# A hybrid decoder step: operands of the chunked recurrence built for four chunks at a time, with wider scans and a decode step by columns

## The chip, the cores and the metric

The kernel runs on one core of a Trainium2 chip. The metric is the device time of one execution in microseconds (us); the kernel before takes 1289.98 us, the median of three runs.

The engines of the core are named as the profile does: PE is TensorE (matmul) and PEld its weight loads, DVE is VectorE, ACT is ScalarE, POOL is GpSimd, SP is SyncE, which here issues most transfers. Each works its own queue in order; semaphores hold an instruction until what it needs is done.

## The reference

One step of a layer with 1024 prompt tokens and 8 decode tokens, model width 1024, 2048 mixed channels. Everything goes through one input projection; three branches read it, and one output projection closes it:

- A: dilated attention, 12 heads of 64, with the three patterns (128,1), (512,4), (2048,16) combined by their softmax denominators; for the decode tokens against a cache of 2048 rows.
- B: a spatial gating unit with chunks of 128 tokens and 8 groups.
- C: a gated linear recurrence of 6 heads with a state of 128 x 128. This is the branch that the change touches:

```python
def body(S, xs):
    qc, kc, vc, gc = xs
    G = jnp.cumsum(gc, axis=1)
    o_inter = jnp.einsum('bchk,bhkv->bchv', qc * jnp.exp(G), S)
    diff = G[:, :, None] - G[:, None, :]
    D = jnp.exp(jnp.where(tri, diff, -jnp.inf))
    A = jnp.einsum('bthk,btshk,bshk->bths', qc, D, kc)
    o = o_inter + jnp.einsum('bths,bshv->bthv', A, vc)
    G_last = G[:, -1]
    S_new = jnp.exp(G_last)[..., None] * S + jnp.einsum(
        'bshk,bshv->bhkv', kc * jnp.exp(G_last[:, None] - G), vc)
    return S_new, o
```

G is the running sum of the logarithms of the forget gate f, k is one minus f. For a decode token the same is one update per head, `S_new = f * S + k v`, and `o = q S_new`.

## The kernel before

The stages run in the order attention, recurrence (`hgrn`), gating unit (`sgu`), output projection. A scheduler that works with estimated times orders the instructions of each engine, so projections of a later head stand among the recurrence of an earlier one. A matmul of the projections is done as three products of rounded parts (high, low); every matmul has the line of the helper `mm` (L100).

`hgrn` goes through three pairs of heads. `c_proj_i` (PSUM tiles `pi`, drained by ACT into V), `c_proj_qf` (tiles `pc`: the part for f drained by ACT at L572, that for q by DVE in `gate`, L152) and `c_proj_z` (tiles `pcz`, drained at L152) are projections. They share two PSUM buffers, so the third product group waits for the drain of the first. `c_head` then works on one head with 1024 tokens in eight chunks of 128:

- It forms G by a running sum for each chunk (L651, eight scans against a tile of ones, which start anew in each chunk), H = G - ln k, eG = exp(G) q (L659).
- For each half of four chunks it transposes k exp(G_last - G) (L667, tile kT), and for each pair of chunks it calls `levels`: for the block widths 32, 8 and 2 a tile T of the `s2` pool with 640 columns, 256 of key operands K (L628) and 384 of query operands Q (L630 differences, L631 exponential on ACT, L633 copy of decays dec on ACT, L634 to L636 products on DVE). The function also makes `last` (L639, L640).
- PE multiplies K and Q of the levels into small blocks of a PSUM tile (`lv`), DVE puts them together in `cmat` (L703 to L710), and PE multiplies this and the state into the output `po`; DVE updates the state S (L721).

`s2` has six tiles. Two calls of `levels` (a half) fill them, and attention uses them for the rounded parts plo and phi of its probabilities (L473, L487). `c_step` is the decode step of a head: for four decode tokens at a time it loads v to all partitions (vb) and the state (ss), and DVE does three multiplications or additions over 512 columns (L752 to L754). `decode` is the attention over the cache for a pair of heads and has its own DVE work on tiles dk, dsc and dmb. GpSimd forms the low parts of the weights (L193).

`sgu` uses one `s2` tile for a bias (bT), and the output projection loads eight tiles of mixed channels y at its start, six of them into `s2`.

## Time and profile before

| what | us |
|---|---|
| median of three runs (1288.97 to 1293.23) | 1289.98 |
| the profiled execution | 1287.74 |
| its span, first to last instruction | 1286.0 |
| TensorE busy (94%) | 1215.2 |
| VectorE busy (71%) | 916.5 |
| ScalarE busy (50%) | 644.2 |
| GpSimd busy (22%) | 285.5 |

The profile is of one execution. A share of busy time is an average over four stages; matmuls are pipelined, so busy time is not peak rate. "Idle before" names the time that an engine stood still ahead of an instruction and what released it. [...]

### The profile page before, as it was taken

How to read it: one execution, taken by the hardware profiler on the slowest of the kernel's cores; microseconds unless marked ns; L12 is line 12 of the kernel's file. 1: busy time of each engine (PE TensorE's matmuls, PEld its weight loads, DVE VectorE, ACT ScalarE, POOL GpSimd, SP SyncE). 2: the span in 40 equal slices, each digit the busy share in tenths (PEclk: the TensorE clock that was granted, in tenths of full speed). 3: DMA queues.
4: the chain of work that ended last, by engine and by line, in shares of the span. 5: the costliest groups of instructions: out<-in, count | busy, mean ns of one | idle time of the engine just before them, and what ended most of it. 6: DMA issues, size and time to landing. Idle time of an engine off the chain costs nothing.

```text
span 1286.0 us, 27698 instructions
## 1 busy us (share of the span) xinstructions
PE 1215.2 (94%) x10610; PEld 1129.3 (88%) x10610; DVE 916.5 (71%) x2427; ACT 644.2 (50%) x1486; POOL 285.5 (22%) x272
## 2 busy tenths in 40 slices
PE   4899989999999999998999989997999999999998
PEld 3899979999899988997888878887889899899998
DVE  5844778668776685879888897889796534664643
ACT  4444444745347554565445554565443242454543
POOL 3532112312123121121011111111011254122221
PEclk9999989999899999999999989999899999999999
DMA  6151032312223123124343424424353224621110
GB/s 234 24 148 54 14 105 62 111 51 59 57 78 107 38 84 89 29 64 107 91 134 96 117 61 134 132 66 106 95 153 95 86 68 134 203 79 46 62 47 29
DMA packets 165045, 114.17 MB, mean 89 GB/s; under 512 B 13945, under 2 KB 158993, under 8 KB 164913
## 3 DMA queue, kind: packets, MB, share of 16 engines
q1 hardware_dynamic: 157520, 110.28, 29.4%
q10 hardware_dynamic: 6816, 1.54, 0.6%
q8 instruction: 83, 1.36, 0.5%
q0 software_dynamic: 576, 0.58, 0.3%
q14 instruction: 50, 0.40, 0.1%
HBM read 84.47 MB, written 22.09 MB: 83 GB/s over the span
## 4 chain that ended last, share of the span: by engine, by line
PE 75%; DVE 15%; DMA 4%; issue 3%; ACT 2%; SPq 0%; POOL 0%; ACTq 0%; DVEq 0%; POOLq 0%
PE po L100 15%; PE pqk L100 10%; PE pv L100 9%; PE paz L100 5%; PE pi L100 5%; PE st L100 4%; PE pbu L100 4%; PE pc L100 4%; PE pbz L100 4%; PE pbv L100 3%; PE pcz L100 2%; PE s L100 2%; DMA dk<-in_cache_k_dram 2%; DVE T L628 2%; DVE T L630 1%
## 5 line engine op out<-in xcount | busy, mean ns | idle before, releaser
L100 PE MATMUL pqk<-wh_qk,h 128*128 128x256 f32 x768 | 157.4, 294 | 5.8 <-ACT h L233 3.0
L100 PE MATMUL pc<-h,wh_cqf 128*128 128x344 f32 x576 | 141.6, 326 | 11.3 <-DVE cz L152 8.0
L100 PE MATMUL po<-woh,yh 128*128 128x256 f32 x512 | 144.1, 282 | 0.5 <-ACT yh L1027 0.5
L100 PE MATMUL po<-woh,yl 128*128 128x256 f32 x512 | 144.2, 282 | 0.0
L100 PE MATMUL po<-wol,yh 128*128 128x256 f32 x512 | 143.4, 280 | 0.0
L100 PEld LDWEIGHTS pqk<-wh_qk,h 128*128 128x128 f32 x768 | 127.8, 197 | 12.3 <-ACT h L233 4.3
L100 PE MATMUL pqk<-wl_qk,h 128*128 128x256 f32 x384 | 113.0, 294 | 0.0
L100 PEld LDWEIGHTS pc<-h,wh_cqf 128*128 128x128 f32 x576 | 100.4, 190 | 14.0 <-DVE cz L152 8.8
L100 PEld LDWEIGHTS po<-woh,yl 128*128 128x128 f32 x512 | 96.2, 188 | 3.0 <-issue 1.7
L100 PEld LDWEIGHTS po<-woh,yh 128*128 128x128 f32 x512 | 96.3, 188 | 2.3 <-ACT yh L1027 2.3
L100 PEld LDWEIGHTS po<-wol,yh 128*128 128x128 f32 x512 | 96.5, 188 | 0.0
L437 DVE CUSTOM_DVE_ANT_0 s<-s,masks 128x512 f32<-128x512 f32 (+2 forms) x144 | 77.6, 578 | 22.7 <-PE s L100 21.7
L100 PE MATMUL pc<-h,wl_cqf 128*128 128x344 f32 x288 | 93.7, 327 | 0.0
L100 PE MATMUL pi<-wh_ci,h 128*128 128x256 f32 x384 | 77.5, 295 | 0.8 <-DVE T L635 0.8
L100 PEld LDWEIGHTS pqk<-wl_qk,h 128*128 128x128 f32 x384 | 75.9, 198 | 1.8 <-issue 0.7
L100 PE MATMUL pv<-wh_v,h 128*128 128x256 f32 x384 | 75.3, 287 | 0.3 <-DVE ss L164 0.3
L100 PE MATMUL pcz<-h,wh_cz 128*128 128x344 f32 x288 | 72.2, 330 | 2.3 <-DVE q L152 2.3
L100 PE MATMUL paz<-h,wh_az 128*128 128x344 f32 x288 | 69.0, 323 | 0.0
L1028 DVE TENSOR_TENSOR yl<-yb,yh 128x512 fp32r<-128x512 f32 x44 | 30.3, 691 | 53.3 <-ACT yh L1027 53.3
L100 PEld LDWEIGHTS pi<-wh_ci,h 128*128 128x128 f32 x384 | 63.5, 198 | 2.7 <-issue 2.4
L100 PEld LDWEIGHTS pv<-wh_v,h 128*128 128x128 f32 x384 | 61.8, 193 | 1.9 <-issue 1.2
L1027 ACT CAST yh<-yb 128x512 fp32r<-128x512 f32 x64 | 39.6, 620 | 43.4 <-PE po L100 43.4
(379 smaller groups left out, 3581.6 us busy)
## 6 DMA issues: line engine op xcount, KB each, us to landing
wro<-in_w_out_dram SPq DMA_DIRECT2D x32, 256.0 KB
wr_qk<-in_w_in_dram SPq DMA_DIRECT2D x48, 128.0 KB
wr_cqf<-in_w_in_dram SPq DMA_DIRECT2D x48, 128.0 KB
dk<-in_cache_k_dram SPq DMA_DIRECT2D x24, 192.0 KB
dv<-in_cache_v_dram SPq DMA_DIRECT2D x24, 192.0 KB
xt<-in_x_prompt_dram SPq DMA_DIRECT2D x8, 512.0 KB
xr<-in_x_prompt_dram SPq DMA_DIRECT2D x32, 128.0 KB
out_o_yp_dram<-xr SPq DMA_DIRECT2D x32, 128.0 KB
```

The source lines that it names most:

```text
L100: nc.tensor.matmul(out, lhsT=lhsT, rhs=rhs, start=start, stop=stop)
L437: nc.vector.tensor_tensor_reduce(out=ps[:, :w], in0=ps[:, :w], in1=nmask[:, S - n + c:S - n + c + w], op0=ALU.add, op1=ALU.max, scale=1.0, ...
L628: nc.vector.tensor_tensor(K.rearrange("p (n w) -> p n w", w=w), g3[:, :, w - 1:w].to_broadcast([P, 4 * n, w]), h3, ALU.subtract)
L630: nc.vector.tensor_tensor(Q[:, 0:3], g4[:, 1:4], g4[:, 0:3, :, w - 1:w].to_broadcast([P, 3, n, w]), ALU.subtract)
L1027: nc.scalar.copy(yh[:, sl, :], y)
L1028: (nc.gpsimd if piece == 0 else nc.vector).tensor_tensor(yl[:, sl, :], y, yh[:, sl, :].bitcast(F32), ALU.subtract)
```

## The change

`levels` takes a half (four chunks) in one call: its tiles have 1280 columns, twice as wide, and each of its instructions works on twice the columns. `lasts` keeps the part that still goes by pairs. The pool `s2` has three tiles of double width in place of six, so attention takes one tile for its two parts, and bT moves to the pool of large tiles (16 buffers). The running sum goes over two chunks with a mask that is 0 at the first column of each chunk in place of the tile of ones. In `c_step`, ACT multiplies vb by a scalar per partition, one decode token at a time, and DVE does the rest as one instruction for each token. The loads of y are five, three of them for two tiles.

```diff
-N_BIG, N_S2, N_S2B, N_PQ, N_W, N_WL, N_GT, N_RAW, N_E = 16, 6, 2, 5, 4, 4, 2, 6, 3
+N_BIG, N_S2, N_S2B, N_PQ, N_W, N_WL, N_GT, N_RAW, N_E = 16, 3, 2, 5, 4, 4, 2, 6, 3
...
-                    plo = s2(f"pl{nm}", F32R)
+                    pl2 = s2(f"pl{nm}", F32R, (P, 2, 512))
+                    plo, phi = pl2[:, 0], pl2[:, 1]
...
-                    phi = s2(f"ph{nm}", F32R)
...
-        def levels(nm, b, q, f, G, H):
+        def levels(nm, b, q, G, H):
...
-                n = 64 // w
-                t = s2(f"T{nm}_{li}", shape=(P, 640))
-                K = t[:, 0:256]
-                Q = t[:, 256:640].rearrange("p (b n w) -> p b n w", b=6, w=w)
+                n = P // w
+                t = s2(f"T{nm}_{li}", shape=(P, 1280))
+                K = t[:, 0:512]
+                Q = t[:, 512:1280].rearrange("p (b n w) -> p b n w", b=6, w=w)
...
-                nc.scalar.activation(t[:, 0:448], t[:, 0:448], AF.Exp)
-                dec = small(f"dec{nm}_{li}", 2 * n, tag="dec").rearrange("p (j n) -> p j n", j=2)
+                nc.scalar.activation(t[:, 0:896], t[:, 0:896], AF.Exp)
+                dec = small(f"dec{nm}_{li}", 2 * n, tag="dec", bufs=1).rearrange("p (j n) -> p j n", j=2)
...
-            for c in range(NT):
-                cs = slice(c * P, (c + 1) * P)
-                nc.vector.tensor_tensor_scan(G[:, cs], ones, G[:, cs], 0.0, ALU.mult, ALU.add)
-                if c % 4 == 3:
-                    cs = slice((c - 3) * P, (c + 1) * P)
+            for c in range(0, NT, 2):
+                cs = slice(c * P, (c + 2) * P)
+                nc.vector.tensor_tensor_scan(G[:, cs], rmask, G[:, cs], 0.0, ALU.mult, ALU.add)
+                if c % 4 == 2:
+                    cs = slice((c - 2) * P, (c + 2) * P)
...
+                T = levels(f"{h}_{half}", b, q, G, H)
                 for c0 in (0, 2):
                     g0 = half * 4 + c0
-                    T, last = levels(f"{h}_{g0}", slice(g0 * P, (g0 + 2) * P), q, f, G, H)
+                    last = lasts(f"{h}_{g0}", slice(g0 * P, (g0 + 2) * P), q, f)
...
-                nc.vector.tensor_tensor(vb, vb, qs[:, 2, bs, None].to_broadcast([P, 4, P]), ALU.mult)
-                nc.vector.tensor_tensor(ss, ss, qs[:, 1, bs, None].to_broadcast([P, 4, P]), ALU.mult)
-                nc.vector.tensor_tensor(ss, ss, vb, ALU.add)
+                for b_ in range(4):
+                    b = 4 * b4 + b_
+                    nc.scalar.activation(vb[:, b_], vb[:, b_], AF.Copy, scale=qs[:, 2, b:b + 1])
+                    nc.vector.scalar_tensor_tensor(ss[:, b_], ss[:, b_], qs[:, 1, b:b + 1], vb[:, b_], ALU.mult, ALU.add)
...
-            bT = s2("bT", shape=(P, 4, P))
+            bT = wk("bT", (P, 4, P))
...
+            for i, n in ((0, 2), (2, 1), (3, 1), (4, 2), (6, 2)):
+                y = s2(f"y{i}", shape=(P, 2, 4, P)) if n == 2 else ee(f"y{i}", (P, 1, 4, P))
```

The order of the instructions moves with it. In the names below the digit behind the letters is the head; T2_4_0 is head 2, pair of chunks from chunk 4, first level, and after the change T2_1_0 is head 2, second half, first level.

VectorE, up to where it drains the second q projection of head 3 (pc3_0_1), which stands among the recurrence of head 2, before:

```order
L582 SCALAR_TENSOR_TENSOR f3_9467<-ft3_2_9557,f3_9467 128x344
L628 TENSOR_TENSOR T2_6_1_9225<-G2_8905,H2_8907 128x256
L630 TENSOR_TENSOR T2_6_1_9225<-G2_8905 128x192
L628 TENSOR_TENSOR T2_6_2_9234<-G2_8905,H2_8907 128x256
L630 TENSOR_TENSOR T2_6_2_9234<-G2_8905 128x192
L703 COPY_PREDICATED cmat_6252<-cmat_6252,lv2_2_9053 128x3x2x8
L640 TENSOR_TENSOR T2_6_q_9243<-f2_8498,q2_8499 128x8x16
L938 TENSOR_REDUCE dmb2_9380<-pmx2_9378 16x1
L156 TENSOR_TENSOR q3_9468<-q3_9468,qt3_0_9585 128x344
L703 COPY_PREDICATED cmat_6252<-cmat_6252,lv2_0_8968 128x2x8
L634 TENSOR_TENSOR T2_4_0_9130<-T2_4_0_9130,q2_8499 128x192
L152 TENSOR_SCALAR q3_9468<-pc3_0_1_9591 128x344
```

The same place after the change; the first row is the drain of the first q projection (pc3_0_0):

```order
L152 TENSOR_SCALAR q3_9242<-pc3_0_0_9334 128x344
L581 SCALAR_TENSOR_TENSOR ft3_0_9325<-k3_9243,f3_9241 128x344
L636 TENSOR_TENSOR T2_0_2_8774<-T2_0_2_8774,dec2_0_2_8778 128x256
L581 SCALAR_TENSOR_TENSOR ft3_1_9328<-k3_9243,f3_9241 128x344
L947 TENSOR_REDUCE dmb2_9154<-pmx2_9152 16x1
L582 SCALAR_TENSOR_TENSOR f3_9241<-ft3_0_9325,f3_9241 128x344
L582 SCALAR_TENSOR_TENSOR f3_9241<-ft3_1_9328,f3_9241 128x344
L948 COPY dmb2_9154<-dmb2_9154 16x128
L581 SCALAR_TENSOR_TENSOR ft3_2_9331<-k3_9243,f3_9241 128x344
L582 SCALAR_TENSOR_TENSOR f3_9241<-ft3_2_9331,f3_9241 128x344
L583 SCALAR_TENSOR_TENSOR k3_9243<-k3_9243,lb1_377,f3_9241 128x1032
L152 TENSOR_SCALAR q3_9242<-pc3_0_1_9365 128x344
```

Before, twenty-nine instructions lie between the two drains, among them twelve operands (L628, L630) of the second half of head 2; after the change ten, and none of these.

VectorE, up to the last drain of the gate projection (pcz1_1_2) at the start of head 2, before:

```order
L628 TENSOR_TENSOR T2_0_2_8956<-G2_8905,H2_8907 128x256
L630 TENSOR_TENSOR T2_0_2_8956<-G2_8905 128x192
L640 TENSOR_TENSOR T2_0_q_8965<-f2_8498,q2_8499 128x8x16
L628 TENSOR_TENSOR T2_2_0_9023<-G2_8905,H2_8907 128x256
L630 TENSOR_TENSOR T2_2_0_9023<-G2_8905 128x192
L628 TENSOR_TENSOR T2_2_1_9032<-G2_8905,H2_8907 128x256
L630 TENSOR_TENSOR T2_2_1_9032<-G2_8905 128x192
L628 TENSOR_TENSOR T2_2_2_9041<-G2_8905,H2_8907 128x256
L630 TENSOR_TENSOR T2_2_2_9041<-G2_8905 128x192
L640 TENSOR_TENSOR T2_2_q_9050<-f2_8498,q2_8499 128x8x16
L659 TENSOR_TENSOR eG2_8906<-eG2_8906,q2_8499 128x1024
L152 TENSOR_SCALAR cz1_1_8716<-pcz1_1_2_8872 128x344
```

And after the change; the first row is the drain in front of it:

```order
L152 TENSOR_SCALAR cz1_1_8538<-pcz1_1_1_8663 128x344
L725 SCALAR_TENSOR_TENSOR S1_6_7894<-S1_5_7839,eL1_7574,ls1_6_7845 128x128
L628 TENSOR_TENSOR T2_0_0_8756<-G2_8727,H2_8729 128x512
L628 TENSOR_TENSOR T2_0_1_8765<-G2_8727,H2_8729 128x512
L630 TENSOR_TENSOR T2_0_1_8765<-G2_8727 128x384
L628 TENSOR_TENSOR T2_0_2_8774<-G2_8727,H2_8729 128x512
L660 COPY eL2_8740<-eG2_8728 128x8
L630 TENSOR_TENSOR T2_0_2_8774<-G2_8727 128x384
L643 TENSOR_TENSOR T2_0_q_8783<-f2_8320,q2_8321 128x8x16
L643 TENSOR_TENSOR T2_2_q_8841<-f2_8320,q2_8321 128x8x16
L725 SCALAR_TENSOR_TENSOR S1_7_7898<-S1_6_7894,eL1_7574,ls1_6_7845 128x128
L152 TENSOR_SCALAR cz1_1_8538<-pcz1_1_2_8694 128x344
```

Eleven narrow operands, of which eight are shown, and the product eG2 stood between the two drains; now five wide ones do, with two updates of the state of head 1, and eG2 stands behind.

ScalarE, where head 2 ends and head 3 begins, before (pdt2s is the cache step, V2_0 and V2_1 drain `pi`):

```order
L602 COPY V2_1_10234<-pi2_0_10235 128x256
L602 COPY V2_0_10233<-pi2_1_10286 128x256
L602 COPY V2_1_10234<-pi2_1_10286 128x256
L724 ACTIVATE csq2_0_9109<-po2_0_8937 128x512
L737 COPY pdt2s_9431<-pda2_9392 128x256
L728 ACTIVATE csq2_0_9109<-pn2_0_9112,eps_69 128x512
L670 COPY kT2_1_9127<-pk2_1_9117 128x512
```

And after the change:

```order
L741 COPY pdt2s_9205<-pda2_9166 128x256
L758 ACTIVATE vb3_0_9784<-vb3_0_9784,qs3_9429 128x128 x4
L758 ACTIVATE vb3_1_9801<-vb3_1_9801,qs3_9429 128x128 x4
L642 COPY T3_0_q_9490<-q3_9242 128x8x32
L642 COPY T3_2_q_9548<-q3_9242 128x8x32
L602 COPY V2_0_9959<-pi2_1_10012 128x256
L602 COPY V2_1_9960<-pi2_1_10012 128x256
```

The eight multiplications of the decode step (two rows of four) now stand here, ahead of two drains of `pi`, which came ahead of the copy pdt2s before.

## Rows read from the trace of the kernel before

**Rows 1.** The page, busy us of each engine, share of the span, instructions.
```profile
PE 1215.2 (94%) x10610; PEld 1129.3 (88%) x10610; DVE 916.5 (71%) x2427; ACT 644.2 (50%) x1486; POOL 285.5 (22%) x272
```

**Rows 2.** Windows by stage: attention with its lead-in, recurrence, and the rest. Columns: stretch, its length, then busy us and (instructions) of PE, PEld, DVE, ACT, POOL; granted clock, DMA share, GB/s.
```profile
0.00:500.00 500.00, 464.38 (x3462) 431.75 (x3463) 350.32 (x895) 254.89 (x562) 123.78 (x139) 0.97 0.29 82
540.00:960.00 420.00, 388.82 (x4147) 354.54 (x4146) 363.50 (x1003) 227.67 (x540) 69.14 (x64) 0.96 0.38 105
960.00:1286.00 326.00, 321.96 (x2739) 304.69 (x2738) 174.32 (x458) 141.54 (x346) 86.29 (x64) 1.00 0.27 85
```

**Rows 3.** Timeline of PE from 540 to 960 us, the rows with over 1 us of idle time ahead. Columns: start, us, engine, line, operation, tiles, shapes, count, and in brackets the idle time ahead and what ended it.
```profile
582.21 0.73 PE L100 MATMUL pc<-h,wh_cqf 128*128 128x344 f32 x2 [2.66 <-DVE cz L152]
...
613.08 0.23 PE L941 MATMUL pmb<-ident,dmb 16*128 16x16 f32 x1 [3.43 <-DVE dmb L939]
...
652.00 0.58 PE L100 MATMUL pc<-h,wh_cqf 128*128 128x344 f32 x2 [2.19 <-ACT V L602]
...
684.29 0.59 PE L100 MATMUL pcz<-h,wh_cz 128*128 128x344 f32 x2 [1.84 <-DVE q L152]
...
727.39 0.58 PE L100 MATMUL pc<-h,wh_cqf 128*128 128x344 f32 x2 [3.02 <-DVE cz L152]
...
754.83 1.89 PE L100 MATMUL pss_ci<-wr_ci,hs 128*8 128x256 f32 x16 [3.68 <-DVE q L152]
...
830.77 0.71 PE L100 MATMUL po<-cmat,V 128*128 128x128 f32 x4 [1.23 <-DVE cmat L710]
...
870.30 0.58 PE L100 MATMUL pc<-h,wh_cqf 128*128 128x344 f32 x2 [2.29 <-DVE cz L152]
...
897.44 1.90 PE L100 MATMUL pss_bv<-wr_bv,hs 128*8 128x256 f32 x16 [3.66 <-DVE q L152]
...
942.27 0.49 PE L100 MATMUL po<-cmat,V 128*128 128x128 f32 x2 [2.08 <-DVE cmat L710]
```

**Rows 4.** Windows of 20 us, columns as in rows 2: the first and the last of the seven from 540 to 960 us whose granted clock is under 1.00.
```profile
580.00:600.00 20.00, 17.79 (x114) 16.77 (x114) 17.33 (x47) 9.53 (x27) 0.00 (x0) 0.91 0.59 148
...
900.00:920.00 20.00, 19.42 (x159) 18.06 (x160) 14.99 (x58) 8.46 (x19) 0.00 (x0) 0.83 0.29 88
```

**Rows 5.** Timeline of DVE at the start of head 0 and of head 2: the scans, and a run of operands up to a drain.
```profile
568.03 2.63 DVE L651 TENSOR_TENSOR_SCAN G<-ones,G 128x128 f32<-128x128 f32 x8 [1.12 <-ACT G L648]
...
723.67 0.42 DVE L628 TENSOR_TENSOR T<-G,H 128x256 f32<-128x256 f32 x1
724.01 0.35 DVE L630 TENSOR_TENSOR T<-G 128x192 f32<-128x192 f32 x1
724.28 0.42 DVE L628 TENSOR_TENSOR T<-G,H 128x256 f32<-128x256 f32 x1
...
725.69 1.22 DVE L659 TENSOR_TENSOR eG<-eG,q 128x1024 f32<-128x1024 f32 x1
726.82 0.51 DVE L152 TENSOR_SCALAR cz<-pcz 128x344 f32<-128x344 f32 x1
```

**Rows 6.** Timeline of DVE from the drain of one q projection of head 3 to the next.
```profile
742.66 0.51 DVE L152 TENSOR_SCALAR q<-pc 128x344 f32<-128x344 f32 x1
...
750.24 1.27 DVE L640 TENSOR_TENSOR T_q<-f,q 128x128 f32<-128x128 f32 x1
...
751.64 1.38 DVE L156 TENSOR_TENSOR q<-q,qt 128x344 f32<-128x344 f32 x1
...
753.02 1.33 DVE L634 TENSOR_TENSOR T<-T,q 128x192 f32<-128x192 f32 x1
754.27 0.50 DVE L152 TENSOR_SCALAR q<-pc 128x344 f32<-128x344 f32 x1
```

**Rows 7.** Timeline of POOL in the same stretch.
```profile
750.00 4.13 POOL L193 TENSOR_TENSOR wl_ci<-wr_ci,wh_ci 128x512 fp32r<-128x512 f32 x3 [26.67 <-ACT wh_ci L192]
```

**Rows 8.** The five lines of operands on DVE by line: count, duration in ns (min/median/max), first and last start, shape; under them the first of the five as a group (busy us, mean ns of one, idle time before).
```profile
L628 DVE TENSOR_TENSOR T<-G,H x72: 404/418/1520, 574.5 to 959.7; 128x256 f32<-128x256 f32 x72
L630 DVE TENSOR_TENSOR T<-G x72: 330/351/1444, 570.6 to 960.1; 128x192 f32<-128x192 f32 x72
L634 DVE TENSOR_TENSOR T<-T,q x72: 281/348/1406, 585.6 to 966.4; 128x192 f32<-128x192 f32 x72
L635 DVE TENSOR_TENSOR T<-T,dec x72: 202/212/1205, 587.3 to 967.1; 128x64 f32<-128x64 f32 x72
L636 DVE TENSOR_TENSOR T<-T,dec x72: 230/280/1378, 590.0 to 967.9; 128x128 f32<-128x128 f32 x72
...
L628 DVE TENSOR_TENSOR T<-G,H 128x256 f32<-128x256 f32 x72 | 34.1, 477 | 1.2 <-PE lv L100 1.2
```

**Rows 9.** By line, columns as in rows 8: a decode multiplication and the state update on DVE; on ACT an activation with 128 columns and an operand per partition, the exponentials of the levels and the copies of decays.
```profile
L754 DVE TENSOR_TENSOR ss<-ss,vb x12: 680/686/737, 544.5 to 933.1; 128x512 f32<-128x512 f32 x12
...
L721 DVE SCALAR_TENSOR_TENSOR S<-S,eL,ls x42: 326/346/350, 592.4 to 996.1; 128x128 f32<-128x128 f32 x42
...
L667 ACT ACTIVATE ki<-H,G x48: 386/393/412, 572.2 to 956.0; 128x128 f32<-128x128 f32 x48
...
L631 ACT ACTIVATE T<-T x72: 558/577/592, 575.4 to 960.5; 128x448 f32<-128x448 f32 x72
...
L633 ACT COPY dec<-T x72: 178/218/256, 582.1 to 965.5; 128x4 f32<-128x4 f32 x24, 128x16 f32<-128x16 f32 x24, 128x64 f32<-128x64 f32 x24
```

**Rows 10.** Waits of PE in the whole span: us in total, times, longest.
```profile
PE s L100 <- DMA QQ<-QQ: 6.9, 3, 2.4
```

More of the change, by code (lines that the diff above doesn't have):

```diff
@@ L636, in levels, with lasts @@
                 nc.vector.tensor_tensor(Q[:, 4:6], Q[:, 1:4:2], dec[:, 0:1, :, None].to_broadcast([P, 2, n, w]), ALU.mult)
-                T.append((K.rearrange("p (c s) -> p c s", c=2), t[:, 256:640].rearrange("p (b c s) -> p c b s", b=6, c=2)))
+                T.append((K.rearrange("p (c s) -> p c s", c=4), t[:, 512:1280].rearrange("p (b c s) -> p c b s", b=6, c=4)))
+            return T
+        def lasts(nm, b, q, f):
             last = ee(f"T{nm}_q", (P, 8, 48))
@@ L641, in levels, with c_head @@
                                                        for x in (f, q)), ALU.mult)
-            return T, last
-        def c_head(h, q, f, kk, qw, V, z, At, lmask, dmask):
+            return last
+        def c_head(h, q, f, kk, qw, V, z, At, lmask, dmask, rmask):
             G, eG, H = (wk(f"{n}{h}") for n in ("G", "eG", "H"))
@@ L766, in hgrn @@
             nc.gpsimd.memset(cm[:, 512:640], 0.0)
+            rmask = cm[:, 872:1000].bitcast(BF16)
+            nc.gpsimd.memset(rmask, 1.0)
+            nc.gpsimd.memset(rmask.rearrange("p (c s) -> p c s", c=2)[:, :, 0:1], 0.0)
             At = [(cm[:, 256 * j:256 * j + 256], cm[:, 512 + 64 * j:576 + 64 * j]) for j in range(2)]
@@ L987, in out_proj @@
             y_v = y_d.rearrange("(k p) s -> p k s", p=P)
-            YT = [s2(f"y{i}", shape=(P, 4, P)) if i < 6 else ee(f"y{i}", (P, 4, P)) for i in range(8)]
-            for i, y in enumerate(YT):
-                nc.sync.dma_start(y, y_v[:, 4 * (i % 3):4 * (i % 3) + 4, (i // 3) * P:(i // 3 + 1) * P])
+            YT = [None] * 8
+            for i, n in ((0, 2), (2, 1), (3, 1), (4, 2), (6, 2)):
+                y = s2(f"y{i}", shape=(P, 2, 4, P)) if n == 2 else ee(f"y{i}", (P, 1, 4, P))
+                nc.sync.dma_start(y.rearrange("p a k s -> p (a k) s"),
+                                  y_v[:, 4 * (i % 3):4 * (i % 3) + 4 * n, (i // 3) * P:(i // 3 + 1) * P])
+                YT[i:i + n] = [y[:, j] for j in range(n)]
             W0 = load_wo(0)
```

8 lines of the change are left out of this document (4 added, 4 removed).

## The prediction

> **What bounds the kernel now.** I read the totals first, then the same by stage, then what ends TensorE's idle time in the stage that the change rewrites. Over the whole span TensorE is busy for 1215.2 of 1286.0 us [rows 1], so only 71 us can be won without removing products, and no product is removed here. By stage [rows 2]: attention (up to 500 us) leaves 36 us idle, and the change leaves its work as it is; the recurrence (540 to 960 us) leaves 31 us, with VectorE busy for 363.5 of 420; what follows leaves 4 us, so an edit there is worth nothing as long as its transfers stay early. The gain has to come out of the recurrence.
>
> There TensorE's long gaps have a pattern [rows 3]. In each even head there are two: one where a projection product waits for VectorE to take the gate projection out of PSUM (2.66, 3.02, 2.29 us), and some 30 us later one where TensorE waits for VectorE around the q projections (3.43 us for dmb of the cache step in head 0; 3.68 and 3.66 us for a drain of q in heads 2 and 4). Odd heads have one each, and the transition to head 2 one that ScalarE ends: 2.19, 1.84, 1.23, 2.08 us. VectorE works its queue in order, and the drain of a projection stands behind operands of the recurrence. [...]
>
> **Operands of a level.** Five VectorE lines, each 72 times, become 36 times at double width: 180 instructions fewer, the same elements. What an instruction costs besides its elements: by durations, two of 256 columns against one of 512 are 2 x 0.418 - 0.686 = 0.15 us [rows 8, 9]; by the pitch of a run without waits, 0.34 and 0.27 us for 256 and 192 columns, hence 0.06 us [rows 5]. So the saving is 11 to 27 us; I take the middle, since operands that wait for ScalarE show their whole duration and the others only the pitch. [...]
>
> **Scans.** Eight of 128 columns run in 2.63 us [rows 5], 0.33 us each; four of 256 save four times the same 0.06 us in six heads, 1.5 us, and 3 us if the whole fixed part counts.
>
> **Decode step.** Three multiplications of 0.69 us [rows 9] twelve times, 25 us, become 48 instructions of 128 columns with a scalar per partition. The nearest row, the state update, takes 0.346 us [rows 9], and by pitch and columns it would be 0.20: 10 to 17 us. VectorE saves 8 to 15 us. ScalarE takes over 48 multiplications, by the nearest row 0.393 us each [rows 9], 19 us. It loses half of its 72 exponentials (0.577) and copies (0.218), whose fixed parts I leave uncounted; it is busy for 227.7 of 420 us [rows 2], so the time itself hides. The wait does not quite: the first of four now holds ScalarE until its load lands, and in head 3 the drains of pi stand right behind eight of them, as the order of ScalarE shows. TensorE then has one more projection of 48 products to do, 5.7 us at 0.12 us apiece by the last stage [rows 2], against 8 x 0.39 = 3.1 us. I price it at nothing, and at 3 us in each of six heads if the load is late.
>
> VectorE loses 21 to 45 us in all, of 363.5.
>
> **Where it falls.** The order of VectorE shows what TensorE feels. Between the drains of the first and second q projection before there are 742.66 to 754.27 = 11.6 us [rows 6], mostly operands of the *next* half written ahead into the second set of tiles. With one set these have to stand behind the drain. Twelve instructions of 0.34 or 0.27 us (3.7 us) and three that a GpSimd subtraction stretches to 1.3 us (4 us) leave this interval: more than the gap of 3.7 us that ends there. So **term a**: the three second gaps, 3.43 + 3.68 + 3.66 = 10.8 us. Ahead of the gate drain eleven narrow operands (6 x 0.34 + 5 x 0.27 = 3.4 us) and the product eG (1.13 us by pitch [rows 5]) become five wide ones (3 x 0.60 + 2 x 0.47 = 2.7 us, estimated from the pitch): 1.8 us less in each of three gaps. **Term b**: 5.4 us. **Term c**: the low clock follows the gaps that go; I take two thirds of 15.6 us, 10.4. **Term d**: the four other gaps, 7.3 us, of which a third, 2.4, because the queue in front of them is shorter by about that share. Together 29.0 us.
>
> **What it costs.** The second set of tiles is gone: the first operand of a half waits until TensorE has read the last product of the half before (levels now reuse all three tiles). From there to the first product that uses them lie 0.60 + 0.47 us, an exponential of under 2 x 0.577, then 0.47 + 0.20 + 0.33 us: about 3 us. TensorE has projections to do meanwhile: the order puts most of a projection group between the halves. I charge a quarter of twelve halves, 9 us, with 0 and 36 us as ends. The attention pairs of tiles, formerly six single ones, hold the same three groups; its order moves a little, and the three waits for copied queries (6.9 us [rows 10]) may grow or shrink by 3 us: nothing taken. bT takes one of sixteen large buffers: four vraw, four U, wn and bT leave six, before it was seven, and three of the four pairs of tiles for the first output weights fit either way. The loads of y become five instead of eight, off any wait that TensorE shows: nothing.
>
> **Sum.** 29.0 - 9 = 20 us off 1287.74 us, the profiled execution (its span and 1.74 us around it), gives 1267.7. That execution lies 2.24 us under the median of the three runs, so the forecast is 1267.7 + 2.2 = 1270 us.
>
> **Rivals.** *The port, not the count.* An instruction of 192 columns took 1.33 us and one of 128 took 1.27 us while GpSimd ran three subtractions in 4.13 us [rows 6, 7]; the longest subtraction of G and H took 1.52 us against a median of 0.418, and the mean is 0.477 [rows 8]. Taken alike for five lines, 360 x 0.06 = 21 us is spent so. It goes with GpSimd's instructions, which stay, so none of it is in my saving; and if the wide operands just meet them elsewhere, ahead of the drains, half of a and b and 3 us of c remain, against 5 of the 9 us charged: 5.4 + 2.7 + 3 - 5 = 6 us, 1284. [...]
>
> *One set of tiles decides.* If projections do not fill the pause between halves, the 3 us above are paid in all twelve, 36 us against 29: slower, 1297. It turns at 29 / 12 = 2.4 us a half. For it: TensorE already ran out of covered work in every head. Against it: it ran out because drains were late, not for want of projections, and these now come earlier.
>
> *The gaps only move.* VectorE was 87% busy in the stage; if TensorE waits for other drains instead, 1290. [...]
>
> **How the numbers follow.** Forecast (1262 to 1279) 0.48; port 0.18; gaps move 0.12; one set of tiles 0.13; everything 0.09. The first, second and last are faster by over 0.3% (3.9 us, about what a measurement of this kernel can tell from no change): 0.75. Same 0.12, slower 0.13. The range leaves out the slower rival and half of the last: 1250 to 1291.
>
> **What would show it.** Right: in the stage VectorE's busy time falls by 21 to 45 us, the waits for q and dmb behind even heads are gone, the granted clock is 1.00 in most windows, the recurrence ends some 20 us sooner. Wrong: new waits of TensorE for operands T or for cmat at the start of second halves; ScalarE idle for vb with drains behind it; the same shortfall of clock in other places; or a gain that appears outside the recurrence, which none of these terms explains.

## The result and the profile after

The changed kernel takes 1302.87 us, the median of nine runs (1294.2 to 1306.59), against 1288.97 for nine runs of the kernel before: a ratio of 1.0104, with a 95% interval of 1.0078 to 1.013. It is slower, outside the range of the forecast. The profiled execution took 1301.46 us, 13.7 more than the profiled one before. Executions of one program differ by nearly as much: of the nine after, the one with the highest granted clock over its span (0.983) took 1294.2 us, the eight others (0.972 to 0.975) 1299.2 to 1306.59 us. What a profile shows of idle time and clock is therefore one sample of its kernel. The granted clock is the share of its full clock that the profile shows TensorE to have had; in both profiles it was 1.00 or 0.50 at a time: before, it was 0.50 from 897 to 906 us and 1.00 from 908 to 912.

The first part of the page, which answers to [rows 1]:

```profile
PE 1227.6 (94%) x10610; PEld 1135.6 (87%) x10610; DVE 887.2 (68%) x2235; ACT 652.8 (50%) x1462; POOL 289.5 (22%) x274
```

VectorE is busy for 29.3 us less, and TensorE for 12.4 us more with the same 10610 instructions, while its idle time over the span grows by 1.3 us only (70.8 to 72.1). The lower granted clock (0.975 over the span against 0.977) makes some 3 of the 12.4 us, an estimate (2.5% of 1299.7 us less 2.3% of 1286.0); the products `pc` of the q and f projections alone are busy for 133.2 us (from 547.3 to 1097.8 us) in place of 124.5 (540.7 to 1085.9 before). The lines that changed, as in [rows 8, 9]: count, duration in ns (min/median/max), first and last start, shape.

```profile
L628 DVE TENSOR_TENSOR T<-G,H x36: 672/684/1781, 592.1 to 960.9; 128x512 f32<-128x512 f32 x36
L630 DVE TENSOR_TENSOR T<-G x36: 540/552/1656, 588.9 to 961.5; 128x384 f32<-128x384 f32 x36
L759 DVE SCALAR_TENSOR_TENSOR ss<-ss,qs,vb x48: 337/346/1382, 549.9 to 922.9; 128x128 f32<-128x128 f32 x48
L758 ACT ACTIVATE vb<-vb,qs x48: 384/388/412, 549.1 to 921.9; 128x128 f32<-128x128 f32 x48
```

So the prices of single instructions came out as taken: 684 ns at 512 columns (0.686 was used), 346 ns for a step of the decode (0.346), 388 ns on ScalarE (0.393). The saving was sized rightly. It did not reach TensorE. Windows by stage, columns as in [rows 2]:

```profile
0.00:500.00 500.00, 458.67 (x3418) 424.00 (x3419) 349.93 (x888) 252.87 (x559) 123.42 (x139) 0.98 0.28 82
540.00:960.00 420.00, 392.75 (x4146) 359.29 (x4144) 342.77 (x842) 238.32 (x525) 74.12 (x67) 0.95 0.38 106
```

In the recurrence VectorE has 20.7 us less to do than before, and TensorE's idle time falls from 31.2 to 27.3 us only. The timeline of PE there, the rows with over 1 us of idle time ahead, as in [rows 3]:

```profile
585.28 0.94 PE L100 MATMUL pc<-h,wh_cqf 128*128 128x344 f32 x2 [4.62 <-DVE cz L152]
...
725.33 0.94 PE L100 MATMUL pc<-h,wh_cqf 128*128 128x344 f32 x2 [2.06 <-DVE cz L152]
...
757.37 0.36 PE L100 MATMUL pi<-wh_ci,h 128*128 128x256 f32 x1 [2.70 <-DVE cmat L707]
...
796.02 0.62 PE L100 MATMUL po<-eG,S 128*128 128x128 f32 x2 [2.31 <-DVE S L725]
...
840.24 0.68 PE L100 MATMUL pcz<-h,wh_cz 128*128 128x344 f32 x2 [2.59 <-DVE q L152]
...
873.49 0.94 PE L100 MATMUL pc<-h,wh_cqf 128*128 128x344 f32 x2 [3.94 <-DVE cz L152]
...
907.72 0.37 PE L100 MATMUL pdn<-dmx,ones 128*128 128x16 f32 x2 [2.28 <-DVE cmat L707]
...
945.64 0.49 PE L100 MATMUL po<-cmat,V 128*128 128x128 f32 x2 [1.35 <-DVE cmat L714]
```

The second gaps of the even heads (q, dmb) are gone, 10.8 us. The gate gaps grew from 7.97 to 10.62 us, and the others (cmat, S, a drain of q in an odd head) from 7.3 to 11.2. The clock fell further: nine windows of 20 us from 540 to 960 us lie under 1.00, and their shortfalls, each times 20 us, make 20.6 us, against 15.6 in the seven before (0.09, 0.09, 0.09, 0.17, 0.08, 0.09 and 0.17; [rows 4] has the first and the last). The first and the last of the nine:

```profile
580.00:600.00 20.00, 15.38 (x88) 14.94 (x81) 18.32 (x28) 10.37 (x25) 3.48 (x5) 0.83 0.62 166
...
940.00:960.00 20.00, 18.31 (x269) 14.92 (x268) 13.35 (x38) 8.19 (x19) 5.66 (x4) 0.83 0.39 115
```

All eight gaps after end in windows under 1.00; of the ten before only five do. The length of a gap did not decide it: the 1.35 us at 945.64 after lie in the last window above, at 0.83, and the 3.02 us at 727.39 before [rows 3] in this one:

```profile
720.00:740.00 20.00, 16.98 (x125) 15.73 (x125) 17.80 (x39) 10.36 (x29) 3.28 (x4) 1.00 0.70 180
```

The largest gap, 4.62 us, is seen from two sides. Timeline of DVE, which still has a drain of the gate projection ahead:

```profile
575.54 0.52 DVE L156 TENSOR_TENSOR cz<-cz,czt 128x344 f32<-128x344 f32 x1
577.97 5.85 DVE L156 TENSOR_TENSOR cz<-cz,czt 128x344 f32<-128x344 f32 x1 [1.91 <-ACT czt L155]
583.74 1.07 DVE L516 TENSOR_TENSOR az<-az,pb 128x512 f32<-128x512 f32 x1
584.72 0.51 DVE L152 TENSOR_SCALAR cz<-pcz 128x344 f32<-128x344 f32 x1
```

and of POOL in the same stretch:

```profile
578.42 2.54 POOL L193 TENSOR_TENSOR wl_cqf<-wr_cqf,wh_cqf 128x512 fp32r<-128x512 f32 x2
580.89 0.12 POOL L775 MEMSET cmat<- 128x2 bf16 x1
580.95 2.48 POOL L193 TENSOR_TENSOR wl_cqf<-wr_cqf,wh_cqf 128x512 fp32r<-128x512 f32 x2
```

The same multiplication takes 0.52 us at 575.54 and 5.85 us while GpSimd does four subtractions with hardly a pause; the drain that frees the PSUM buffer stands behind it. The stretch is part of this gap, but not what made it grow. A gap is the time from the end of the last gate product to the end of its drain, less the time for which TensorE has other products meanwhile. In head 0, before (from 574.06 to 582.16, other products until 579.55) and after (from 579.59 to 585.23, until 580.67):

```profile
573.74 0.32 PE L100 MATMUL pcz<-h,wl_cz 128*128 128x344 f32 x1
...
579.17 0.38 PE L740 MATMUL pdt0s<-ident,pdt0ss 128*128 128x128 f32 x2
...
581.65 0.50 DVE L152 TENSOR_SCALAR cz<-pcz 128x344 f32<-128x344 f32 x1
```

```profile
579.27 0.32 PE L100 MATMUL pcz<-h,wl_cz 128*128 128x344 f32 x1
...
580.09 0.58 PE L100 MATMUL pc<-h,wh_cqf 128*128 128x344 f32 x2
```

Read so for the three even heads, in us, before / after:

| head | last gate product to end of its drain | other products of TensorE meanwhile | gap |
|---|---|---|---|
| 0 | 8.10 / 5.64 | 5.49 / 1.08 | 2.66 / 4.62 |
| 2 | 8.45 / 7.22 | 5.48 / 5.22 | 3.02 / 2.06 |
| 4 | 8.15 / 7.59 | 5.92 / 3.71 | 2.29 / 3.94 |

VectorE's drains come 4.3 us sooner in sum, stretched operations included; TensorE has 6.9 us less to do meanwhile, since its own order moved too. The subtractions meet the operands in both kernels: in head 2 they take 1.43 to 1.52 us at 719.31, 720.67 and 722.11 before (192 or 256 columns), and 1.65 and 1.77 us at 719.21 and 720.78 after (384 and 512 columns).

Part of the loss lies ahead of the recurrence. The first product of the gate projection starts at 540.7 us before and at 547.3 after; the last product of pbu in the gating unit at 1085.9 and 1097.8. So 6.6 us are lost in attention, 5.3 between these two, and the rest of the 13.7 behind them. Windows of attention: before, after, and in the run sep told below.

```profile
60.00:540.00 480.00, 465.09 (x3444) 433.59 (x3445) 338.34 (x871) 245.06 (x531) 105.56 (x115) 0.98 0.25 71
```

```profile
60.00:540.00 480.00, 459.88 (x3405) 426.96 (x3406) 332.86 (x855) 240.14 (x522) 104.32 (x114) 0.98 0.25 71
```

```profile
60.00:540.00 480.00, 465.28 (x3437) 433.07 (x3438) 336.83 (x868) 243.56 (x527) 105.12 (x115) 0.98 0.25 71
```

TensorE does 5.2 us less there at the same clock. The waits of PE show four waits for copied queries where [rows 10] had three, a longer one for nat (1.1 us before) and a new one for az:

```profile
PE s L100 <- DMA QQ<-QQ: 8.9, 4, 2.6
...
PE pqk L100 <- DVE nat L304: 2.2, 2, 1.1
PE paz L100 <- DVE az L152: 1.6, 1, 1.6
```

### The profile page after: what moved, and what is told of

Its sections match the earlier page's. It is cut to its first block, busy times and chain, and to the rows that moved or that the text cites. A ratio compares the mean times of both kernels' runs of the same rounds, so it can differ in the third digit from the quotient of the medians.

```text
span 1299.7 us, 27452 instructions
## 1 busy us (share of the span) xinstructions
PE 1227.6 (94%) x10610; PEld 1135.6 (87%) x10610; DVE 887.2 (68%) x2235; ACT 652.8 (50%) x1462; POOL 289.5 (22%) x274
## 4 chain that ended last, share of the span: by engine, by line
PE 77%; DVE 12%; DMA 5%; issue 3%; ACT 2%; SPq 0%; POOL 0%; DVEq 0%; ACTq 0%; POOLq 0%
PE po L100 16%; PE pqk L100 10%; PE pv L100 9%; PE pc L100 7%; PE paz L100 5%; PE st L100 4%; PE pbu L100 4%; PE pbz L100 4%; PE pi L100 3%; PE pcz L100 3%; PE pbv L100 3%; DMA dk<-in_cache_k_dram 2%; PE s L100 2%; PE lv L100 1%; DMA xt<-in_x_prompt_dram 1%
## 5 line engine op out<-in xcount | busy, mean ns | idle before, releaser
L100 PE MATMUL pqk<-wh_qk,h 128*128 128x256 f32 x768 | 153.0, 289 | 6.5 <-DVE nat L304 2.2
L100 PE MATMUL pc<-h,wh_cqf 128*128 128x344 f32 x576 | 146.9, 337 | 10.6 <-DVE cz L152 10.6
L100 PEld LDWEIGHTS pqk<-wh_qk,h 128*128 128x128 f32 x768 | 125.0, 193 | 12.5 <-DVE nat L304 2.7
L100 PEld LDWEIGHTS pc<-h,wh_cqf 128*128 128x128 f32 x576 | 105.0, 199 | 12.8 <-DVE cz L152 11.5
L100 PE MATMUL pc<-h,wl_cqf 128*128 128x344 f32 x288 | 96.4, 337 | 1.6 <-POOL wl_cqf L193 1.1
L437 DVE CUSTOM_DVE_ANT_0 s<-s,masks 128x512 f32<-128x512 f32 (+2 forms) x144 | 77.8, 577 | 28.6 <-PE s L100 27.3
```

The lines of the kernel that those rows point to most:

```text
L100: nc.tensor.matmul(out, lhsT=lhsT, rhs=rhs, start=start, stop=stop)
L437: nc.vector.tensor_tensor_reduce(out=ps[:, :w], in0=ps[:, :w], in1=nmask[:, S - n + c:S - n + c + w], op0=ALU.add, op1=ALU.max, scale=1.0, ...
```

## The experiments

Three theories stood against each other. *Order*: VectorE's total is not what TensorE waits for; another order of the queues makes other gaps, and the changed kernel got a worse one (a worse draw), in attention too. *One set*: with three tiles a half waits for the half before. *Port*: GpSimd's subtractions stretch VectorE's operations, and wide ones no less (the name is the author's for what holds them, which no run shows). The table has all runs: the ratio to the kernel before with its interval, and from each profile VectorE's busy time, TensorE's busy time in attention (60 to 540 us), its idle time and granted clock from 560 to 980 us (420 less its busy time). Attention has the "pairs" of tiles of the change, or "single" ones in two ways: before's, or a pool of its own.

| run | ratio | DVE | attention | PE, 60-540 | idle, 560-980 | clock |
|---|---|---|---|---|---|---|
| before | 1 | 916.5 | single | 465.1 | 30.8 | 0.96 |
| after | 1.0104 (1.0078 to 1.013) | 887.2 | pairs | 459.9 | 27.3 | 0.95 |
| sep | 1.005 (1.0034 to 1.0067) | 887.4 | single | 465.3 | 33.7 | 0.96 |
| pool | 1.0063 (1.0038 to 1.0087) | 912.9 | pairs | 461.5 | 31.1 | 0.96 |
| narrow | 1.0059 (1.0035 to 1.0084) | 895.6 | pairs | 460.6 | 26.1 | 0.97 |
| scandec | 1.0072 (1.0043 to 1.0102) | 898.1 | single | 464.4 | 30.0 | 0.96 |
| dec | 1.0003 (0.9988 to 1.0019) | 890.7 | single | 464.0 | 29.0 | 0.98 |
| scan | 1.008 (1.0052 to 1.0109) | 917.2 | single | 464.3 | 38.7 | 0.95 |
| sepwide | 1.017 (1.0147 to 1.0193) | 897.3 | single | 464.3 | 38.7 | 0.96 |
| sepnarrow | 1.0037 (1.0016 to 1.0059) | 914.0 | single | 466.2 | 32.5 | 0.96 |
| sepnodec | 1.0019 (0.9999 to 1.0039) | 897.9 | single | 464.8 | 30.2 | 0.98 |
| nolowbefore | 0.9887 (0.986 to 0.9913) | 877.9 | single | 464.1 | 17.8 | 0.99 |
| nolowafter | 0.9936 (0.9914 to 0.9959) | 860.5 | pairs | 461.5 | 16.9 | 0.98 |
| dvelowbefore | 1.0044 (1.0025 to 1.0063) | 917.4 | single | 464.7 | 28.4 | 0.97 |
| order_b1 | 0.9983 (0.9965 to 1.0002) | 915.8 | single | 464.7 | 25.7 | 0.98 |
| order_b2 | 1.0051 (1.0031 to 1.0071) | 913.6 | single | 464.3 | 31.2 | 0.97 |
| order_a1 | 1.0088 (1.0061 to 1.0116) | 881.9 | pairs | 459.8 | 27.5 | 0.96 |
| order_a2 | 1.0038 (1.0012 to 1.0063) | 890.0 | pairs | 460.6 | 29.4 | 0.97 |
| sep_order1 | 1.0063 (1.0044 to 1.0082) | 888.0 | single | 464.8 | 32.2 | 0.97 |
| dec_order1 | 1.0063 (1.004 to 1.0085) | 903.6 | single | 464.3 | 31.7 | 0.97 |

**Attention's tiles.** sep is the changed kernel with six single tiles for attention, in a pool that closes before the three wide ones open; pool is the kernel before with the change's tiles alone; narrow is the changed kernel with operands by pairs of chunks, side by side in the wide tiles. The edits of sep and of narrow:

```diff
-                    pl2 = s2(f"pl{nm}", F32R, (P, 2, 512))
-                    plo, phi = pl2[:, 0], pl2[:, 1]
+                    plo = s2(f"pl{nm}", F32R)
...
+        with tc.tile_pool(name="s2a", bufs=1) as pa:
+            pool2[:] = [pa, 2 * N_S2]
...
+        with tc.tile_pool(name="s2w", bufs=1) as pw:
+            pool2[:] = [pw, N_S2]
```

```diff
-                n = P // w
-                t = s2(f"T{nm}_{li}", shape=(P, 1280))
+                n = 64 // w
+                if len(made) <= li:
+                    made.append(s2(f"T{nm}_{li}", shape=(P, 1280)))
+                t = made[li][:, o:o + 640]
```

> The changed kernel with one part undone: attention has its six single tiles back (a pool of its own, closed before the recurrence), the recurrence keeps its three wide ones. Order theory (one tile for the two parts rearranges attention): the recurrence's first gate product starts at 541 us as before, not 547, and some 7 of the 14 us are won back, about 1296 us. One-set theory (the recurrence lacks its second set of tiles): no gain over the changed kernel, 1303 us, and TensorE's idle time from 540 to 960 us stays at 27 us. Port theory (GpSimd's subtractions hold wide operands up): the start moves back too, but the gate drain of head 0 can still be held up; 1296 to 1300 us.

> The kernel before with the tiles of the change alone: three wide tiles in the pool, one for attention's two parts, bT and y as changed; operands stay narrow and by pairs (two pairs share a wide tile), scans and decode step as before. Order theory: the recurrence starts 6 to 7 us late, 1295 to 1297 us. One-set theory: late starts of second halves with no saving against them, 1300 to 1310 us. Port theory: narrow operands meet the subtractions as before, so only attention's part is lost, 1293 to 1297 us.

> The changed kernel with operands by pairs again, each half the width, in the same three wide tiles; scans, decode step, attention and loads as changed. VectorE gets some 11 to 27 us back on. Order theory: the same late start; 1300 to 1306 us, so width itself is worth little. One-set theory: operands of the first pair can go ahead of the second, so waits shrink; under 1300 us. Port theory: stretched operands are shorter ones; 1298 to 1303 us.

In all six profiles with pairs TensorE is busy for 459.8 to 461.5 us in attention, in all others for 464.0 to 466.2. The two groups do not touch, and pool, which leaves attention's instructions as they are, is in the first: the pairs of tiles cost attention 2.5 to 6.4 us, from the nearest to the farthest profiles of the groups. TensorE's idle time ahead of the first gate product divides the runs alike: 39.7 to 42.3 us with pairs, 35.6 to 38.1 without. That this is the order can be read from the traces: TensorE's products up to there come in one order in all kernels with pairs and in another in all with single tiles, and the two part after 801 products (nolowbefore, nolowafter and dvelowbefore leave the order of their group only after some 3500). In the time, sep is 0.54% below the changed kernel, 7.0 us, as the order theory had it, and pool's 1297.5 us lie close to its range. With operands of half width in the changed kernel (narrow) the time falls too, to 1295.6 us, while VectorE does 8.4 us more; that is under the ranges of order and port, and only the one-set theory had it.

**Scans and decode step alone.** scandec, dec and scan are the kernel before with those hunks of the change's diff, and nothing else of it.

> The kernel before with the scans over two chunks and the decode step by columns, all tiles and operands as before. VectorE loses about 10 to 18 us. Order theory: attention's order is as before, so no loss; 1284 to 1290 us. If saved VectorE time never reaches TensorE (gaps move): 1289 us within 4. If ScalarE's new wait for vb holds drains: 1292 to 1296 us, with TensorE waiting for V or k behind ScalarE.

> The kernel before with the decode step by columns of scalars alone. Order theory (the shorter queue of VectorE is used up because other instructions come late in it): VectorE's busy time falls by some 10 us, TensorE's idle time in the recurrence stays within 3 us of 31.2, and the time lies between 1.000 and 1.005 of before. ScalarE theory (the multiplications of vb hold ScalarE's queue until the load lands, and copies that TensorE waits for stand behind them): it alone carries most of the 1.007 that scans and decode step together cost, so 1.004 to 1.009, with gaps of TensorE that ScalarE ends. Port theory: as many operations as before on VectorE that GpSimd can stretch, so no change beyond the 10 us saved: 0.993 to 1.000.

> The kernel before with the scans over two chunks alone. The decode step alone measured no change (1.0003) and scans with decode step together 1.0072. Order theory: a saving of 2 to 3 us on VectorE is only a new draw of the queue's order, so anywhere from 0.997 to 1.007, with TensorE's idle time in the recurrence within 5 us of 31.2 and attention unchanged (first gate product at 541 to 543 us). A theory of cost (a scan of 256 columns holds VectorE for 0.67 us in one piece and delays what stands behind): 1.004 or more. The prediction's saving with no other effect: 0.998 to 1.000.

In dec VectorE's busy time falls by 25.8 us and the time stays (1.0003). Not all of the 25.8 us is work that went: the decode step's own lines fall by 8.0 us (26.4 to 18.4), and the five lines of operands, which the edit leaves as they are, by 10.0 (135.3 to 125.3), with 12 instructions over 1 us in place of 21. The scans cost 0.8%. No scan of the changed kernel takes over 0.69 us; in scan the median is the same, 672 ns, but some are stretched, up to 1764, and its 24 scans take 19.1 us where 48 took 16.2. Its profile has 38.7 us of idle time, with waits that before has not in this size, for cmat, a drain of q, and GpSimd's weights. Waits of PE from 540 to 1000 us in scan (total, times, longest):

```profile
PE po L100 <- DVE cmat L710: 8.4, 3, 6.2
PE pi L100 <- DVE q L152: 7.6, 2, 4.7
PE pc L100 <- POOL wl_cqf L193: 6.8, 5, 2.4
```

The 2.9 us more of scans do not make up these waits by themselves. By its range 1.008 fits a cost of wide scans (1.004 or more) and lies just outside that of order (to 1.007); against such a cost speaks that the same scans gain in the next runs. scandec, at 1300.3 us, lies above all that was expected of it. That ScalarE's multiplications hold up TensorE did not show in dec.

**Back from one set of tiles to the change.** sepnarrow is the kernel before with the double tiles alone (attention kept); sepwide adds wide operands, sepnodec the scans to that, and sep the decode step.

> The kernel before with one thing changed: the operands of a half lie in three double tiles instead of six single ones (attention keeps its six in a pool of its own); every instruction of the operands keeps its width, scans and decode step are as before. Against the run with wide operands in the same tiles (1.017): if one set of tiles is what costs there, 1.010 or more here; if the wide operands cost it (a burst of the double length ahead of drains), 1.000 to 1.006 here. Order theory: 0.999 to 1.006.

> The changed kernel with attention's six single tiles in a pool of their own, closed before the recurrence, and without the new scans and the new decode step: what is left of the change are the wide operands in one set of three tiles. Order theory: attention ends where it ended before (first product of the gate projection at 541 to 543 us), the recurrence keeps 28 to 34 us of idle time, 0.999 to 1.004 of before. One-set theory (each half waits until the half before has been read): the recurrence is 5 to 12 us longer than before's 545.3 and waits of TensorE for lv or cmat grow; 1.005 to 1.010. The prediction's own terms a to d without the charge, if scans and decode step were what spoiled them: 0.985 to 0.992.

> The changed kernel with attention's own pool and without the new decode step: wide operands and wide scans. Between the run without both (1.017) and the run with both (1.005). If the decode step is what shortens VectorE's queue where it matters, 1.012 to 1.018; if the two are worth what they save in VectorE's time (2 us and 10 us), 1.013 to 1.016; order theory: anywhere between 1.003 and 1.018, in no proportion to the time saved.

1.0037, 1.017, 1.0019, 1.005: the scans cost 0.8% on the kernel before and gain 1.5% here. The parts have no price of their own that adds up. sepwide, 22 us slower, lies above every range that was expected of it, and what it loses stays open. sepnarrow lies within what order alone does (below): with narrow operands one set of tiles costs some 4.8 us, 7.6 at the upper end of the interval, and the 36 us of the rival are excluded. No run has wide operands with two sets.

**GpSimd's subtractions.** In nolowbefore and nolowafter GpSimd writes zeros where it formed the low parts of the recurrence's weights (q and f, i, gate), so the products run with those parts left out. In dvelowbefore the subtractions of q and f move to VectorE.

```diff
-                nc.gpsimd.tensor_tensor(lo, raw, hi.bitcast(F32), ALU.subtract)
+                if nm[0] == "c":
+                    nc.gpsimd.memset(lo.bitcast(F32), 0.0)
+                else:
+                    nc.gpsimd.tensor_tensor(lo, raw, hi.bitcast(F32), ALU.subtract)
```

```diff
-                nc.gpsimd.tensor_tensor(lo, raw, hi.bitcast(F32), ALU.subtract)
+                (nc.vector if nm[:3] == "cqf" else nc.gpsimd).tensor_tensor(lo, raw, hi.bitcast(F32), ALU.subtract)
```

> The kernel before, with the low parts of the weights of the recurrence's projections (q and f, i, gate) set to zero by GpSimd in place of GpSimd's subtraction, so that the products are those of the high part alone; the products themselves all run. Port theory (subtractions with two operands on GpSimd stretch VectorE's operations, and drains come late by it): VectorE's busy time falls by 10 to 21 us and the time by 5 to 12 us, 0.990 to 0.996. Order theory: the gaps have their cause in what stands ahead of the drains, so the time falls by 0 to 4 us, 0.997 to 1.000. One-set theory says nothing on this kernel.

> The changed kernel with the same omission: low parts of the recurrence's weights set to zero, all products kept. Port theory: the change gains here what it was meant to, 10 us or more against the kernel before with the same omission, so a ratio of 0.980 to 0.987 to the plain kernel before; the gaps at the gate drains (4.62, 2.06, 3.94 us) go. Order theory: it stays as far above the kernel before with the same omission as the change lies above the kernel before, 8 to 13 us. One-set theory: likewise 5 to 13 us above, with waits at the start of the halves.

> The kernel before with the low parts of the weights of the q and f projections (24 of the 48 subtractions of the recurrence) formed on VectorE in place of GpSimd. Port theory: GpSimd's 24 subtractions of 1.39 us no longer stretch anything, VectorE's busy time grows by less than the 24 x 0.69 = 16.5 us of the work itself, the gaps at the gate drains shrink as they did without the subtractions, and the time is 0.994 to 1.001. Order theory (only what is queued on VectorE counts): 16 us more in its queue, 1.004 to 1.010.

The page of nolowbefore, of nolowafter and of dvelowbefore:

```profile
PE 1211.0 (95%) x10610; PEld 1122.4 (88%) x10610; DVE 877.9 (69%) x2427; ACT 643.7 (51%) x1486; POOL 244.9 (19%) x272
```

```profile
PE 1215.9 (95%) x10610; PEld 1128.9 (88%) x10610; DVE 860.5 (67%) x2235; ACT 650.0 (51%) x1462; POOL 246.3 (19%) x274
```

```profile
PE 1220.7 (94%) x10610; PEld 1130.8 (87%) x10610; DVE 917.4 (71%) x2451; ACT 647.6 (50%) x1486; POOL 257.6 (20%) x248
```

Without 48 subtractions the kernel before gains 14.6 us by its ratio, and the changed one 21.7 (1.0104 to 0.9936): no edit of VectorE's own work took as much off either of them. The gate gaps are gone in both; what is left is waits for q in the one and, in their place, for cmat and V in the other. Waits of PE from 540 to 1000 us, nolowbefore and nolowafter:

```profile
PE pbv L100 <- DVE q L152: 3.7, 1, 3.7
PE pi L100 <- DVE q L152: 3.1, 1, 3.1
```

```profile
PE pbv L100 <- DVE cmat L710: 6.6, 1, 6.6
PE pi L100 <- ACT V L605: 3.5, 1, 3.5
```

So the port theory is right that the gate gaps go with the subtractions. The change costs 1.04% with them and 0.50% without (0.9936 over 0.9887), a difference no larger than what order alone does (below), so the port's share of the loss is not shown. It is not right that the change then gains what it was meant to (0.980 to 0.987 was expected): the recurrence is as idle as that of nolowbefore, 16.9 and 17.8 us. Nor was any theory right in size: nolowbefore lies just under the port's range (0.990 to 0.996), and nolowafter 6.4 us above it, where order had 8 to 13. Zeros also come sooner than differences (0.53 against 1.3 to 1.4 us each), so stretching and late weights are not taken apart here, nor is what products with zeros do to the clock (0.98 and 0.99 in the table). In dvelowbefore half of the subtractions are on VectorE at 0.68 us each, 16.3 us, and its busy time rises by 0.9. The gate gaps shrink to 1.1 us there, as the port theory expected, but the time rises by 0.44%, out of its range and into that of order (1.004 to 1.010): TensorE waits for other things, from 540 to 1000 us above all for these:

```profile
PE po L100 <- DVE cmat L710: 5.0, 2, 2.9
PE pc L100 <- DVE wl_cqf L193: 3.9, 5, 1.4
```

**Order alone.** In order_b1 and order_a1 the differences for Q and for K of a level are written in the other order; in order_b2 and order_a2 the logarithm for H behind that for G (b: kernel before, a: changed kernel). No instruction is added, left out or resized. sep_order1 and dec_order1 are sep and dec with the first swap.

```diff
+                nc.vector.tensor_tensor(Q[:, 0:3], g4[:, 1:4], g4[:, 0:3, :, w - 1:w].to_broadcast([P, 3, n, w]), ALU.subtract)
                 nc.vector.tensor_tensor(K.rearrange("p (n w) -> p n w", w=w), g3[:, :, w - 1:w].to_broadcast([P, 4 * n, w]),
                                         h3, ALU.subtract)
-                nc.vector.tensor_tensor(Q[:, 0:3], g4[:, 1:4], g4[:, 0:3, :, w - 1:w].to_broadcast([P, 3, n, w]), ALU.subtract)
```

```diff
-            nc.scalar.activation(H[:, :S], kk[:, :S], AF.Ln, bias=tiny)
             nc.vector.tensor_scalar(G[:, :S], f[:, :S], 2.0 ** -63, None, ALU.max)
             nc.scalar.activation(G[:, :S], G[:, :S], AF.Ln)
+            nc.scalar.activation(H[:, :S], kk[:, :S], AF.Ln, bias=tiny)
```

> The kernel before, with the two differences of a level (for Q and for K) written in the other order: the same instructions, on the same tiles, only another order of the queues from the first half of head 0 on. Order theory: the kernel before is a good draw, and another order of the same work costs 0.2 to 1%, with other gaps of TensorE in the recurrence (30 to 40 us in sum). Resource theories (VectorE's time, the port, the set of tiles): nothing changes, 0.998 to 1.002.

> The kernel before, with the logarithm for H written behind the one for G: the same instructions, another order of the queues. Order theory: as in the run above, 0.2 to 1% off the kernel before and not the same gaps. Resource theories: 0.998 to 1.002.

> The changed kernel, with the two differences of a level written in the other order: the same instructions, another order of the queues. Order theory: as likely faster as slower than the changed kernel, anywhere from 1.000 to 1.016 of the kernel before. Resource theories: as the changed kernel, 1.008 to 1.013.

> The changed kernel, with the logarithm for H written behind the one for G: the same instructions, another order of the queues. Order theory: anywhere from 1.000 to 1.016, and not the gaps of the changed kernel (4.62 us at 581, 3.94 us at 870). Resource theories: 1.008 to 1.013.

> The changed kernel with attention's six single tiles in a pool of their own, and the two differences of a level in the other order. Order theory with the loss in attention as the one lasting cost of the change: against the changed kernel with the same swap (1.0088) it gains the 4 to 6 us by which attention ends sooner, so 1.003 to 1.006 if the recurrence drew the same, and 0.996 to 1.008 since it draws again. One-set theory: the set is as small as in the changed kernel, so 1.005 or more.

> The kernel before with the two edits that did not cost anything: the decode step by columns (1.0003) and the two differences of a level in the other order (0.9983). If edits added up, 0.998 to 0.999. Order theory: no sum, 0.994 to 1.006; a result under 0.997 would be a version that beats both kernels, and then by its draw of the order, not by the work that it saves.

The instructions of before take 0.9983 to 1.0051 of its time in three orders, those of the change 1.0038 to 1.0104: 0.7% within each (8.8 us), more than the 0.5% between the middles of the two ranges. Order by order the change costs 1.04%, 1.05% (order_a1 over order_b1) and -0.13% (order_a2 over order_b2), so three orders do not say what it costs on average. Of the two swaps the second moves either kernel beyond its interval; order_b1, which the order theory had as slower, and order_a1 lie also where the theories of a resource had them (0.998 to 1.002 and 1.008 to 1.013). Waits of PE from 540 to 1000 us in order_b1 and in order_b2:

```profile
PE pi L100 <- DVE q L152: 3.6, 2, 2.9
PE pbv L100 <- DVE q L152: 3.4, 1, 3.4
```

```profile
PE pi L100 <- DVE q L152: 6.0, 1, 6.0
PE pbv L100 <- ACT vraw L829: 3.5, 2, 2.2
PE pbv L100 <- DVE q L152: 3.5, 1, 3.5
PE pmb L941 <- DVE dmb L939: 3.4, 1, 3.4
```

The same kinds of gaps come and go with a swap of two statements. dec_order1 bears it out by missing a sum: dec (1.0003) and the swap (0.9983) make 1.0063 together. sep_order1 is 0.25% below order_a1, but their intervals overlap, so what attention's tiles gained in sep (0.54%) is not shown a second time. No run beats the kernel before beyond its interval, except those that leave work out.

## Why the prediction was wrong

- **VectorE loses 21 to 45 us**: right, 29.3, with the durations of single instructions as taken: 684 ns measured at 512 columns, where 0.686 us was used, and 552 ns at 384.
- **Term a**, 10.8 us of second gaps: these gaps went, as the order said. But the time came back as waits for cmat, S and a later drain of q, so **term d** (2.4 us gained) turned into 3.9 us lost.
- **Term b**, 5.4 us: wrong in sign, 2.65 us lost. VectorE's side came out near it: the three drains end 4.3 us sooner after the last gate product. What the step held fixed was TensorE's own work ahead of the wait, and that shrank by 6.9 us. Its durations were those of an undisturbed run [rows 5], while GpSimd's subtractions stretch operands in the same place in both kernels. The rival *The port, not the count* had this place: without the subtractions (nolowbefore, nolowafter) the gate gaps go in either kernel. That the subtractions made the gaps grow is not shown. What the trace shows is the stretch: one multiplication took 5.85 us through four subtractions.
- **Term c**, 10.4 us of clock, two thirds of the 15.6 us of shortfall before: no run shows this term; in its place the two profiles show 5.0 us lost (20.6 against 15.6). The term let the low clock go in step with the gaps; before, five of ten gaps end in windows at 1.00, after none of eight, and the runs do not show what decides it.
- **Charge of 9 us** for one set of tiles: sepnarrow has some 4.8 us for it (7.6 at the upper end), with narrow operands; no wait of TensorE for T of 1 us stands in the profile after.
- **Attention, nothing taken**: wrong by 6.6 us at its end, and shown by sep and pool. That the pairs "hold the same three groups" is true of space; the order that comes with them costs TensorE.

By gaps and clock the recurrence comes out 0.8 us worse (4.2 us gained, 5.0 lost), where 29 were to be won. The step that failed is *Where it falls*: it priced the gaps of one order as if the new order would have those gaps less something, with TensorE's own order unmoved. *The gaps only move* (1290) was the rival for the recurrence; with 7 us of attention it is 1297, and the rest, 6 us, is of the size of a draw (8.8 us between order_b1 and order_b2), which does not show that it is one. What stays open is whether wide operands have a lasting cost: 1.017, 1.0019, 1.005 and 1.0063 with them in one set and attention restored (sepwide, sepnodec, sep, sep_order1) all lie above 1 and spread further than order showed on the kernel before. Some 4.5 us of the 5.3 lost from the first gate product to the last of pbu are neither gaps nor clock. 32 products of the output projection (2.8 us) now stand ahead of the last of pbu, though the stage behind is no shorter for it; the rest was not traced.

## What to carry to other kernels

Where an engine is waited for at a few drains, its total is no currency: 25.8 us less busy time on VectorE (dec) were worth nothing, and two orders of the same instructions lie 8.8 us apart. A gap has two sides: besides when the drain comes, ask what the waiting engine still has to do by then, since a new order moves both. Before a part of a change is believed to have a price, run it in two or three orders with the same instructions; differences under 0.7% here were within what order alone did. And look for what disturbs the waited-for engine: without GpSimd's 48 subtractions TensorE's idle time in the recurrence fell from 30.8 to 17.8 us, which no edit of VectorE's own work came near.

## What the runs showed of the hardware

One VectorE operation on two SBUF operands was held by several GpSimd instructions in a row: 5.85 us against a median of 516 ns, through four subtractions. Operations of the same 344 columns that read PSUM were not stretched at all in the same kernel: twelve of the drains at L152 ran while GpSimd subtracted, and none took over 0.52 us. Lines of DVE after the change (ns min/median/max):

```profile
L156 DVE TENSOR_TENSOR cz<-cz,czt x18: 499/516/5847, 559.3 to 885.1; 128x344 f32<-128x344 f32 x18
```

```profile
L152 DVE TENSOR_SCALAR cz<-pcz x18: 503/514/518, 555.6 to 872.9; 128x344 f32<-128x344 f32 x18
```

And stretching is larger than the 21 us that five lines had shown: VectorE's busy time falls by 38.6 us (916.5 to 877.9) when 48 subtractions go, without an instruction of its own less, 0.80 us for each.

The granted clock did not go by the length of a gap here, nor was it the same in every execution: 1.00 in the window with a gap of 3.02 us before, 0.83 in the one with 1.35 us after, and 0.972 to 0.983 over the span in nine executions of the changed kernel.
